# One sum of each feed-forward group made by an adding DMA transfer, and two more groups with a fourth step by seven

## The chip, the cores and the metric

The kernel runs on one core of a Trainium2 chip. The time is the device time of one execution in microseconds, taken as the median of three runs of the kernel before: 1799.47 us (1798.95 to 1800.05). Lower is better. A core has a matrix engine (TensorE, PE), VectorE (DVE), ScalarE (ACT), GpSimd (POOL), the sync engine that issues transfers (SyncE, SP), and 16 DMA engines that move data between memory (HBM) and the on-chip buffer (SBUF). TensorE accumulates into PSUM banks.

## What is computed

Two decoder layers over one sequence of 256 tokens of width 2048, in float32. Layer 0 mixes tokens by causal trailing means, layer 1 by differential attention. After each stands a dense feed-forward part, and that is where the change is:

```python
D_MODEL, SEQ, D_FF = 2048, 256, 5632

def swiglu(h, wg, wu, wd):
    return (jax.nn.silu(h @ wg) * (h @ wu)) @ wd

for i in range(2):
    h = h + mix(i, rmsnorm(h, norm_mix[i]))
    h = h + swiglu(rmsnorm(h, norm_ffn[i]), w_gate[i], w_up[i], w_down[i])
return rmsnorm(h, final_norm)
```

All weights are read from HBM once: three matrices of 2048 x 5632 in each of the two feed-forward parts, besides those of the mixers.

## The kernel before

**Precision.** Each operand is split into two halves, `hi` (the value rounded to the format that TensorE multiplies fast) and `lo` (what is left). A product is three matmuls: hi by hi, hi by lo, lo by hi. For weights ScalarE makes `hi` by a cast (L349 `whi`, L363 `thi`) and VectorE makes `lo` by a subtraction (L350 `wlo`, L364 `tlo`).

**Groups and steps.** `group()` computes one block of 256 x 1024 outputs. It runs over steps; a step is 256 rows of the weights by 1024 columns, stored in HBM as four blocks of 128 x 512 for each of 128 partitions in the order B12, B11, B22, B21 (1024 KB). A plain step is eight block products, 24 matmuls of 128 x 512. A **step by seven** replaces the eight products by seven products of sums (the Strassen-Winograd scheme), 21 matmuls. For that the weights have to be summed first, by `sums()` on VectorE:

- L355: `tsum0` = the pair (B11, B22) + B12, 128 x 1024
- L356: `tsum1[0]` = `tsum0[0]` + B22
- L357: `tsum1[1]` = `tsum1[0]` + B21

Then `tsum0` and `tsum1` are split like the weights (two L363 on ScalarE, two L364 on VectorE), and three of the four raw blocks by L349 and L350 (B12 is not used by itself). `prepared()` does all of this for one step: load, sums, halves. `products()` (L416) issues the matmuls, and `combined()` (L437 to L447) adds up the banks at the end of a group.

**Buffers.** `raw`, `whi` and `wlo` have three buffers each; `tsum0` and `tsum1` have one each, in the pool of the feed-forward part (`hp`). So a step by seven can write `tsum0` only when the one before it has been read by L356, L363 and L364.

**Loops.** `ffn(layer, ...)` runs over three chunks of 4, 4 and 3 gate/up groups. A gate/up group has eight steps over the 2048 inputs and gives 512 columns of gate and 512 of up; `GATE_UP[layer][g]` names its steps by seven. After each chunk follow two down groups of 8, 8 and 6 steps, whose steps by seven are 2, 4 and 6 as far as they go. The very last down group of layer 1 has none. The gate/up groups of both layers have the steps 2, 4, 5, 6 or 2, 4, 6 by seven; only the first of layer 0 has 4 and 6.

**Order.** The program isn't run in the order in which it is written. `in_order_of_need()` takes all instructions as `Step`s with a cost (`holds`: how long the engine is taken; `lasts`: how long until the result is there), walks them through the engines with a rank by need, up to eight times, keeps the shortest plan and fixes the order of TensorE, VectorE, ScalarE and SyncE by it. GpSimd's instructions stay in the order of the program. The costs are constants in the code: a load by SyncE holds it for 330 ns and lands after 2100 ns and 2500 ns per MiB, one transfer behind another. Each engine then executes its instructions strictly in the planned order; the one that waits holds up all behind it on its engine.

All weight loads go through SyncE's queue (L343), as do the transposing transfers of the activations (L515). GpSimd does nothing but a few set-up instructions at the start.

Of the kernel before, what the change touches and what calls it, by code (L numbers as in the profile page):

```python
# [10 lines left out]
F32 = mybir.dt.float32  # L11
# [3 lines left out]
ALU = mybir.AluOpType  # L15
# [3 lines left out]
P = 128  # L19
# [23 lines left out]

SEVEN = (2, 4, 5, 6)
SEVEN_DOWN = (2, 4, 6)
GATE_UP = [[(4, 6), (2, 4, 5, 6), (2, 4, 6), (2, 4, 5, 6), (2, 4, 5, 6), (2, 4, 5, 6), (2, 4, 6), (2, 4, 6), (2, 4, 5, 6), (2, 4, 5, 6), (2, 4, 6)], [(2, 4, 6), (2, 4, 5, 6), (2, 4, 6), (2, 4, 5, 6), (2, 4, 5, 6), (2, 4, 5, 6), (2, 4, 6), (2, 4, 6), (2, 4, 5, 6), (2, 4, 5, 6), (2, 4, 6)]]
SEVEN_QKV = (2, 4, 6)

EARLY = (tuple(range(NP)), (4, 6))
# [4 lines left out]
B12, B11, B22, B21 = range(4)  # L54
# [6 lines left out]
PE, DVE, ACT, SP, POOL = (mybir.EngineType.PE, mybir.EngineType.DVE, mybir.EngineType.Activation,  # L61
                          mybir.EngineType.SP, mybir.EngineType.Pool)
# [3 lines left out]
LANDING = 2100  # L66
# [4 lines left out]
class Step:  # L71

    def __init__(self, k, ins=None):
        self.k, self.ins, self.engine = k, ins, ins.engine if ins else POOL
        turns = bool(ins) and ins.opcode == "DmaTransposeAnt"
        self.dma = turns or bool(ins) and ins.opcode == "DMACopy"
        self.before, self.after, self.reads = set(), [], set()
        if not ins:
            self.holds = self.lasts = 0
            return  # L80
        size = lambda ap: math.prod(c for _, c in list(ap.ap)[1:])
        n = max(size(a) for a in list(ins.outs) + list(ins.ins) if hasattr(a, "ap"))
        if turns:
            self.share = TURN_TILE * n * P / 2048
            self.holds, self.lasts = 1290, 1000 + self.share
        elif self.dma:
            bytes_ = 4 * math.prod(c for _, c in ins.outs[0].ap)
            self.share = PER_MIB * bytes_ / 2 ** 20
            self.holds, self.lasts = (60 if self.engine == ACT else 330), LANDING + self.share
        elif self.engine == PE:  # L90
            n = size(ins.outs[0])
            one = 110 if ins.is_transpose else 14 + n / 2.4 if "float32r" in str(ins.ins[0].dtype) else 14 + n / 0.6
            self.holds, self.lasts = one, one + 163
        elif self.engine == DVE:
            if ins.opcode == "TensorScalarPtr":
                self.lasts = 185 + n / 0.96 if n > 8 else 159
            else:
                self.lasts = 152 + n / (1.92 if ins.opcode == "TensorCopy" else 0.96)
            self.holds = max(self.lasts - 80, 60)
        elif self.engine == ACT:  # L100
            self.lasts = 165 + n * 0.852
            if ins.opcode == "Activation" and any(hasattr(a, "ap") for a in list(ins.ins)[1:]):
                self.lasts += 100
            self.holds = max(self.lasts - 30, 60)
            if len(list(ins.ins[0].ap)) > 3:
                self.lasts += 80
            if len(ins.outs) > 1:
                self.lasts, self.holds = self.lasts + 190, self.lasts + 160
        else:
            self.holds = self.lasts = 400  # L110
# [168 lines left out]
def trunk_kernel(ctx, tc, x_n, gains, scale_in, final_in, subln, lam_in, band, counts_in, dist,  # L279
# [10 lines left out]
    nc = tc.nc  # L290
# [10 lines left out]
    def bank(i, shape=(P, 512)):  # L301
        return psum.tile(list(shape), F32, name=f"b{i}", tag=f"b{i}")
# [35 lines left out]
        return ap.bitcast(F32)  # L338


    def load(src):
        raw = wraw.tile([P, 4, 512], F32, name="raw")
        nc.sync.dma_start(out=raw, in_=src)  # L343
        return raw

    def halves(raw, lo_block=0):
        hi = whl.tile([P, 4, 512], F32R, name="whi")
        lo = whl.tile([P, 4, 512], F32R, name="wlo")
        nc.scalar.copy(hi[:, lo_block:], raw[:, lo_block:])  # L349
        nc.vector.tensor_tensor(lo[:, lo_block:], raw[:, lo_block:], f32(hi[:, lo_block:]), ALU.subtract)  # L350
        return hi, lo

    def sums(pool, raw):
        s, t = (pool.tile([P, 2, 512], F32, name=f"tsum{i}") for i in range(2))
        nc.vector.tensor_tensor(s, raw[:, B11:B22 + 1], raw[:, B12:B12 + 1].broadcast_to([P, 2, 512]), ALU.add)  # L355
        nc.vector.tensor_tensor(t[:, 0], s[:, 0], raw[:, B22], ALU.add)  # L356
        nc.vector.tensor_tensor(t[:, 1], t[:, 0], raw[:, B21], ALU.add)  # L357
        return s, t

    def sum_halves(pool, t, bufs, i):  # L360
        hi = pool.tile([P, 2, 512], F32R, name=f"thi{i}", bufs=bufs)
        lo = pool.tile([P, 2, 512], F32R, name=f"tlo{i}", bufs=bufs)
        nc.scalar.copy(hi, t)  # L363
        nc.vector.tensor_tensor(lo, t, f32(hi), ALU.subtract)  # L364
        return hi, lo
# [5 lines left out]
    def group(steps, pool, by_bank=0, bufs=1):  # L371


        plan = []
        for n, (a, seven, src) in enumerate(steps):
            if seven and n + 1 < len(steps) and steps[n + 1][1]:
                plan.append([(P5, [(S1, 1, 0)]), (M7, [(S3, 1, 1)]), (M6, [(S2, 2, 0)]), (P4, [(A22, 2, 1)]),
                             (M1, [(A11, 0, B11)]), (M2, [(A12, 0, B21)]), (P3, [(S4, 0, B22)])])
            elif seven:
                plan.append([(M1, [(A11, 0, B11)]), (M2, [(A12, 0, B21)]), (P3, [(S4, 0, B22)]), (P5, [(S1, 1, 0)]),  # L380
                             (M7, [(S3, 1, 1)]), (M6, [(S2, 2, 0)]), (P4, [(A22, 2, 1)])])
            else:
                plan.append([(C11, [((0, 0), 0, B11), ((1, 0), 0, B21)]), (C12, [((0, 0), 0, B12), ((1, 0), 0, B22)]),
                             (C21, [((0, 1), 0, B11), ((1, 1), 0, B21)]), (C22, [((0, 1), 0, B12), ((1, 1), 0, B22)])])
        left = {}
        for step in plan:
            for b, parts in step:
                left[b] = left.get(b, 0) + 3 * len(parts)
        ps = {}

        def prepared(seven, src):
            raw = load(src)
            t = sums(pool, raw) if seven else None
            w = [halves(raw, B11 if seven else 0)]
            if seven:
                w += [sum_halves(pool, t[i], bufs, i) for i in range(2)]
            return w

        def products(a, seven, w, b, parts):
            first = b not in ps  # L400
            if first:
                ps[b] = bank(b)
            for at, which, block in parts:
                hi, lo = w[which]
                if seven:
                    ah, al = a[:, 0, at], a[:, 1, at]
                else:
                    k, t = at
                    if a.shape[2] == 8:
                        slot = ((A11, A21), (A12, A22))[k][t]  # L410
                        ah, al = a[:, 0, slot], a[:, 1, slot]
                    else:
                        ah, al = (a[:, k, i, t * P:(t + 1) * P] for i in range(2))
                for x, y in ((ah, hi), (ah, lo), (al, hi)):
                    left[b] -= 1
                    nc.tensor.matmul(ps[b], x, y[:, block], start=first, stop=(left[b] == 0))  # L416
                    first = False

        head = len(steps) - by_bank
        for (a, seven, src), step in zip(steps[:head], plan[:head]):  # L420
            w = prepared(seven, src)
            for b, parts in step:
                products(a, seven, w, b, parts)
        if by_bank:
            ws = [prepared(seven, src) for a, seven, src in steps[head:]]
            for n in range(len(plan[head])):
                for (a, seven, src), step, w in zip(steps[head:], plan[head:], ws):
                    products(a, seven, w, *step[n])
        return ps
# [126 lines left out]
    with tc.tile_pool(name="start", bufs=1, reuse_waits="tile") as st:  # L556
# [27 lines left out]
        load_w(1, 0)  # L584
        load_w(1, 1)
        w_pool.append(load(pool_w[2]))
        nc.sync.dma_start(out=band_raw, in_=band)
        w_pool.append(load(pool_w[3]))
# [144 lines left out]
    def ffn(layer, xq, ss, next_op, next_gain):  # L733
# [3 lines left out]
        with tc.tile_pool(name=f"ffn{layer}", bufs=1, reuse_waits="tile") as hp:  # L737
            g0 = 0
            ys = []
            for c, n in enumerate(CHUNKS):  # L740
# [6 lines left out]
                for g in range(g0, g0 + n):  # L747

                    by_seven = GATE_UP[layer][g]
                    cs = combined(group([(xq[p], p in by_seven, w_gu[layer][g, p]) for p in range(NP)], hp), hp)  # L750
# [50 lines left out]
    with tc.tile_pool(name="attn", bufs=1, reuse_waits="tile") as ap_, ExitStack() as heads:  # L801
# [70 lines left out]
        for g in range(4):  # L872

            order, by_seven = LATE if g else EARLY
# [17 lines left out]
        for g in range(2):  # L892
            order, by_seven = LATE if g else EARLY
# [120 lines left out]
```

## Time and profile before

| | |
|---|---|
| median of three runs | 1799.47 us |
| the profiled execution, its time | 1799.01 us |
| its span, first to last instruction | 1797.2 us |
| granted TensorE clock, mean | 0.998 |
| L416 matmuls | 7491 |
| steps, of these by seven | 328, 127 |
| weight loads of 1024 KB by SyncE (L343) | 330 |

The page gives the busy time of each engine as a share of the span. A busy TensorE is not TensorE at its peak; how many matmuls start in a stretch of time says more, and who ended TensorE's waits says where another engine was late. A row of a group reads: line, engine, operation, output from inputs, shapes, count, then busy us and mean ns of one, then the idle time before it and what ended that.

### The profile page before, as it was taken

The page shows a single profiled execution, that of the slowest core. Times are in us where ns is not written, and L with a number is a line of the kernel's source. Part 1 is how long each engine was busy: PE and PEld are TensorE (multiplying, and loading weights), DVE is VectorE, ACT ScalarE, POOL GpSimd, SP SyncE. Part 2 cuts the span into 40 slices and gives each one's busy share as a digit, 9 for nine tenths or more (in the row PEclk, how much of TensorE's full clock was granted, in tenths as well). Part 3 has the DMA queues.
Part 4 walks back from the last instruction along what each step waited for, and adds up shares of the span by engine and source line. Part 5 has one row for each costly group of instructions (what it writes and reads, how often), then busy time and mean ns, then how long its engine had stood idle before and what let it go on. Part 6 is the DMA issues. An engine that isn't in the chain of part 4 may idle for free. (4 is left out here: it accounts for less than half of the span.)

```text
span 1797.2 us, 20952 instructions
## 1 busy us (share of the span) xinstructions
PE 1782.2 (99%) x7945; PEld 1467.4 (82%) x7945; DVE 1680.4 (94%) x1876; ACT 1184.0 (66%) x1294; POOL 0.7 (0%) x6
## 2 busy tenths in 40 slices
PE   9999999999999999999999999999999999999997
PEld 7888888888888888888888888888788888888886
DVE  7999999999999999998987889999999999999996
ACT  7676755666645678766666777676755766655773
POOL 0000000000000000000000000000000000000000
PEclk9999999999999999999999999999999999999999
DMA  7556655566655667644554464665655666566663
GB/s 267 211 204 223 226 208 193 199 243 203 223 209 204 206 201 231 215 175 164 187 186 174 179 199 176 216 230 198 223 213 207 210 214 227 206 223 215 217 211 117
DMA packets 105844, 369.99 MB, mean 206 GB/s; under 512 B 61072, under 2 KB 61200, under 8 KB 63376
## 3 DMA queue, kind: packets, MB, share of 16 engines
q1 hardware_dynamic: 104880, 367.03, 58.7%
q10 hardware_dynamic: 864, 1.63, 0.2%
q8 instruction: 62, 1.02, 0.2%
q14 instruction: 38, 0.31, 0.1%
HBM read 352.90 MB, written 2.10 MB: 198 GB/s over the span
## 5 line engine op out<-in xcount | busy, mean ns | idle before, releaser
L416 PE MATMUL b<-whi,xp 128*128 128x512 f32 x2654 | 849.3, 392 | 0.5 <-ACT e L529 0.2
L349 ACT CAST whi<-raw 128x1536 fp32r<-128x1536 f32 (+1 forms) x328 | 572.3, 1746 | 255.6 <-PE b L416 219.9
L350 DVE TENSOR_TENSOR wlo<-raw,whi 128x1536 fp32r<-128x1536 f32 (+1 forms) x328 | 681.6, 2078 | 55.5 <-ACT whi L349 53.8
L416 PEld LDWEIGHTS b<-whi,xp 128*128 128x128 f32 x2654 | 497.4, 188 | 103.7 <-ACT e L529 0.6
L416 PE MATMUL b<-wlo,xp 128*128 128x512 f32 x1327 | 519.8, 392 | 1.2 <-DVE wlo L350 1.2
L363 ACT CAST thi<-tsum 128x1024 fp32r<-128x1024 f32 x254 | 266.2, 1051 | 186.3 <-DVE tsum L355 61.5
L416 PE MATMUL b<-whi,h 128*128 128x512 f32 x1108 | 348.2, 389 | 0.7 <-DVE c L444 0.4
L364 DVE TENSOR_TENSOR tlo<-tsum,thi 128x1024 fp32r<-128x1024 f32 x254 | 306.2, 1217 | 4.9 <-ACT thi L363 4.6
L416 PEld LDWEIGHTS b<-wlo,xp 128*128 128x128 f32 x1327 | 249.3, 188 | 53.5 <-DVE wlo L350 2.8
L416 PE MATMUL b<-thi,xp 128*128 128x512 f32 x744 | 254.5, 389 | 0.0
L416 PEld LDWEIGHTS b<-whi,h 128*128 128x128 f32 x1108 | 207.9, 188 | 44.6 <-DVE c L444 0.9
L416 PE MATMUL b<-wlo,h 128*128 128x512 f32 x554 | 215.7, 389 | 0.0
L416 PEld LDWEIGHTS b<-thi,xp 128*128 128x128 f32 x744 | 139.6, 188 | 29.1
L355 DVE TENSOR_TENSOR tsum<-raw 128x1024 f32<-128x1024 f32 x127 | 154.5, 1216 | 1.5 <-DMA raw<-w_gu 1.5
L416 PE MATMUL b<-tlo,xp 128*128 128x512 f32 x372 | 145.0, 390 | 0.6 <-DVE tlo L364 0.6
L416 PEld LDWEIGHTS b<-wlo,h 128*128 128x128 f32 x554 | 104.0, 188 | 21.8 <-DVE wlo L350 0.2
L356 DVE TENSOR_TENSOR tsum<-tsum,raw 128x512 f32<-128x512 f32 x127 | 86.7, 683 | 0.4
L357 DVE TENSOR_TENSOR tsum<-tsum,raw 128x512 f32<-128x512 f32 x127 | 86.7, 683 | 0.2
L416 PEld LDWEIGHTS b<-tlo,xp 128*128 128x128 f32 x372 | 69.8, 188 | 16.0 <-DVE tlo L364 1.7
L416 PE MATMUL b<-thi,h 128*128 128x512 f32 x240 | 79.6, 389 | 0.0
L416 PE MATMUL b<-whi,oT 128*128 128x512 f32 x216 | 68.6, 394 | 0.0
L416 PEld LDWEIGHTS b<-thi,h 128*128 128x128 f32 x240 | 45.0, 188 | 9.4
(154 smaller groups left out, 1276.3 us busy)
## 6 DMA issues: line engine op xcount, KB each, us to landing
raw<-w_gu SPq DMA_DIRECT2D x176, 1024.0 KB, 4.9
raw<-w_down SPq DMA_DIRECT2D x88, 1024.0 KB, 4.8
raw<-w_qk SPq DMA_DIRECT2D x32, 1024.0 KB, 4.9
raw<-w_v SPq DMA_DIRECT2D x16, 1024.0 KB, 4.9
raw<-w_o SPq DMA_DIRECT2D x16, 1024.0 KB, 5.0
x_tok<-x_n SPq DMA_DIRECT2D x4, 512.0 KB, 7.3
w<-pool_w SPq DMA_DIRECT2D x4, 512.0 KB, 7.6
raw<-pool_w SPq DMA_DIRECT2D x2, 1024.0 KB, 11.7
```

The costliest lines, as they stand in the source:

```text
L349: nc.scalar.copy(hi[:, lo_block:], raw[:, lo_block:])
L350: nc.vector.tensor_tensor(lo[:, lo_block:], raw[:, lo_block:], f32(hi[:, lo_block:]), ALU.subtract)
L355: nc.vector.tensor_tensor(s, raw[:, B11:B22 + 1], raw[:, B12:B12 + 1].broadcast_to([P, 2, 512]), ALU.add)
L356: nc.vector.tensor_tensor(t[:, 0], s[:, 0], raw[:, B22], ALU.add)
L357: nc.vector.tensor_tensor(t[:, 1], t[:, 0], raw[:, B21], ALU.add)
L363: nc.scalar.copy(hi, t)
L364: nc.vector.tensor_tensor(lo, t, f32(hi), ALU.subtract)
L416: nc.tensor.matmul(ps[b], x, y[:, block], start=first, stop=(left[b] == 0))
```

## The change

In a feed-forward group the first step by seven no longer makes `tsum0` on VectorE. SyncE copies B12 twice from HBM into the two halves of `tsum0`, and GpSimd issues a transfer that reads B11 and B22 from HBM and adds them to what lies there. The load of `raw` leaves B12 out. L356 and L357 stay on VectorE. The later steps by seven of a group are as before, and so are all groups outside the feed-forward parts (their pool has another name).

Two gate/up groups of layer 0, 2 and 7, get a fourth step by seven, step 5. The planner learns the cost of a transfer issued by GpSimd: twice the time on the wire, 1100 ns for the issue, 1000 ns more until it lands.

```diff
-GATE_UP = [[(4, 6), (2, 4, 5, 6), (2, 4, 6), (2, 4, 5, 6), (2, 4, 5, 6), (2, 4, 5, 6), (2, 4, 6), (2, 4, 6), (2, 4, 5, 6), (2, 4, 5, 6), (2, 4, 6)], [
+GATE_UP = [[(4, 6), (2, 4, 5, 6), (2, 4, 5, 6), (2, 4, 5, 6), (2, 4, 5, 6), (2, 4, 5, 6), (2, 4, 6), (2, 4, 5, 6), (2, 4, 5, 6), (2, 4, 5, 6), (2, 4, 6)], [
...
             self.share = PER_MIB * bytes_ / 2 ** 20
-            self.holds, self.lasts = (60 if self.engine == ACT else 330), LANDING + self.share
+            if self.engine == POOL:
+                self.share *= 2
+            self.holds = {ACT: 60, POOL: 1100}.get(self.engine, 330)
+            self.lasts = LANDING + self.share + (1000 if self.engine == POOL else 0)
...
-    def load(src):
+    def load(src, first=0):
         raw = wraw.tile([P, 4, 512], F32, name="raw")
-        nc.sync.dma_start(out=raw, in_=src)
+        nc.sync.dma_start(out=raw[:, first:], in_=src[:, first:])
         return raw
...
-    def sums(pool, raw):
-        s, t = (pool.tile([P, 2, 512], F32, name=f"tsum{i}") for i in range(2))
-        nc.vector.tensor_tensor(s, raw[:, B11:B22 + 1], raw[:, B12:B12 + 1].broadcast_to([P, 2, 512]), ALU.add)
+    def sums(pool, raw, ready):
+        s = ready or pool.tile([P, 2, 512], F32, name="tsum0")
+        t = pool.tile([P, 2, 512], F32, name="tsum1")
+        if not ready:
+            nc.vector.tensor_tensor(s, raw[:, B11:B22 + 1], raw[:, B12:B12 + 1].broadcast_to([P, 2, 512]), ALU.add)
...
+    def sums_by_transfer(pool, src):
+        s = pool.tile([P, 2, 512], F32, name="tsum0")
+        nc.sync.dma_start(out=s, in_=src[:, B12:B12 + 1].broadcast_to([P, 2, 512]))
+        nc.gpsimd.dma_start(out=s, in_=src[:, B11:B22 + 1], accum_op=ALU.add)
+        return s
...
-        def prepared(seven, src):
-            raw = load(src)
-            t = sums(pool, raw) if seven else None
+        def prepared(seven, src, first=False):
+            by_transfer = seven and first
+            ready = sums_by_transfer(pool, src) if by_transfer else None
+            raw = load(src, B11 if by_transfer else 0)
+            t = sums(pool, raw, ready) if seven else None
...
-            w = prepared(seven, src)
+            first = pool.name.startswith("ffn") and seven and src is next(s for _, by_seven, s in steps if by_seven)
+            w = prepared(seven, src, first)
```

More of the change, by code (lines that the diff above doesn't have):

```diff
@@ L45 @@
 SEVEN_DOWN = (2, 4, 6)
-GATE_UP = [[(4, 6), (2, 4, 5, 6), (2, 4, 6), (2, 4, 5, 6), (2, 4, 5, 6), (2, 4, 5, 6), (2, 4, 6), (2, 4, 6), (2, 4, 5, 6), (2, 4, 5, 6), (2, 4, 6)], [(2, 4, 6), (2, 4, 5, 6), (2, 4, 6), (2, 4, 5, 6), (2, 4, 5, 6), (2, 4, 5, 6), (2, 4, 6), (2, 4, 6), (2, 4, 5, 6), (2, 4, 5, 6), (2, 4, 6)]]
+GATE_UP = [[(4, 6), (2, 4, 5, 6), (2, 4, 5, 6), (2, 4, 5, 6), (2, 4, 5, 6), (2, 4, 5, 6), (2, 4, 6), (2, 4, 5, 6), (2, 4, 5, 6), (2, 4, 5, 6), (2, 4, 6)], [(2, 4, 6), (2, 4, 5, 6), (2, 4, 6), (2, 4, 5, 6), (2, 4, 5, 6), (2, 4, 5, 6), (2, 4, 6), (2, 4, 6), (2, 4, 5, 6), (2, 4, 5, 6), (2, 4, 6)]]
 SEVEN_QKV = (2, 4, 6)
```

## The prediction

> **What bounds the kernel now.** The order of reading is: the busy line, the stretches of the two feed-forward layers, who keeps TensorE waiting, then whom VectorE waits for. The first fence has the busy line of the page and two rows of the view of stretches (columns: PE, PEld, DVE, ACT, POOL, each busy us and count; granted clock; DMA share; GB/s).
>
> ```profile
> span 1797.2 us, 20952 instructions
> PE 1782.2 (99%) x7945; PEld 1467.4 (82%) x7945; DVE 1680.4 (94%) x1876; ACT 1184.0 (66%) x1294; POOL 0.7 (0%) x6
> ...
> 57.00:722.00 665.00, 664.75 (x2933) 549.40 (x2932) 642.61 (x639) 442.95 (x420) 0.00 (x0) 1.00 0.62 214
> 1086.00:1745.00 659.00, 656.70 (x2899) 541.90 (x2899) 633.17 (x634) 425.99 (x399) 0.00 (x0) 1.00 0.61 211
> ```
>
> In the first layer TensorE starts 2933 matmuls in 665 us, one per 0.227 us, at full clock, and is short of work for 0.25 us. So TensorE is the bound, and it issues at an even beat; VectorE is busy for 97% of the same stretch and is the engine that would be the bound next. The waits of TensorE's weight loads, and three stretches of 50 us, show where VectorE comes too late:
>
> ```profile
> PEld b L416 <- DVE wlo L350: 2.9, 6, 1.4
> PEld b L416 <- DVE tlo L364: 1.7, 4, 1.0
> PEld b L416 <- DVE c L444: 1.4, 2, 0.9
> ...
> 350.00:400.00 50.00, 49.75 (x219) 40.67 (x218) 49.38 (x49) 36.36 (x35) 0.00 (x0) 1.00 0.68 236
> ...
> 1100.00:1150.00 50.00, 49.00 (x223) 40.41 (x222) 50.00 (x58) 33.59 (x38) 0.00 (x0) 1.00 0.57 211
> ...
> 1250.00:1300.00 50.00, 48.94 (x214) 39.50 (x213) 50.00 (x53) 36.34 (x35) 0.00 (x0) 1.00 0.66 218
> ```
>
> All waits of TensorE for VectorE's halves and combinations come to 6.0 us, a third of a per cent. That is nearly all there is to win besides matmuls. The chain that ended last crosses VectorE (L350, L442, L355, L444) at 1267 to 1272 us, and then runs on TensorE alone for 417 us:
>
> ```profile
> 1267.35 2.20 DVE wlo L350
> 1269.55 0.60 DVE c L442
> 1270.15 0.06 DVE tsum L355
> 1270.21 0.99 issue
> 1271.21 0.69 DVE c L444
> 1271.90 0.04 issue
> 1271.95 417.20 PE b L416 x1838
> ```
>
> **What the change removes.** The groups of VectorE, shapes apart, and one of TensorE that reads their result:
>
> ```profile
> L350 DVE TENSOR_TENSOR wlo<-raw,whi 128x2048 fp32r<-128x2048 f32 x201 | 459.4, 2285 | 46.4 <-ACT whi L349 45.2
> L364 DVE TENSOR_TENSOR tlo<-tsum,thi 128x1024 fp32r<-128x1024 f32 x254 | 306.2, 1217 | 4.9 <-ACT thi L363 4.6
> L350 DVE TENSOR_TENSOR wlo<-raw,whi 128x1536 fp32r<-128x1536 f32 x127 | 222.2, 1750 | 9.1 <-ACT whi L349 8.6
> L355 DVE TENSOR_TENSOR tsum<-raw 128x1024 f32<-128x1024 f32 x127 | 154.5, 1216 | 1.5 <-DMA raw<-w_gu 1.5
> L416 PE MATMUL b<-tlo,xp 128*128 128x512 f32 x372 | 145.0, 390 | 0.6 <-DVE tlo L364 0.6
> L356 DVE TENSOR_TENSOR tsum<-tsum,raw 128x512 f32<-128x512 f32 x127 | 86.7, 683 | 0.4
> ```
>
> Feed-forward groups with a step by seven: layer 0 has 11 gate/up and 6 down, layer 1 has 11 and 5 (its last has none): 33. Each loses one L355: 33 x 1.22 = 40 us of VectorE. Back to back an instruction costs about 0.08 us less than it lasts, as the starts of these rows show (2.20 between the first two, 2.27 for the two tlo of the second):
>
> ```profile
> 1380.96 2.29 DVE L350 TENSOR_TENSOR wlo<-raw,whi 128x2048 fp32r<-128x2048 f32 x1
> 1383.16 2.35 DVE L364 TENSOR_TENSOR tlo<-tsum,thi 128x1024 fp32r<-128x1024 f32 x2
> 1385.43 2.28 DVE L350 TENSOR_TENSOR wlo<-raw,whi 128x2048 fp32r<-128x2048 f32 x1
> ...
> 1393.56 1.22 DVE L355 TENSOR_TENSOR tsum<-raw 128x1024 f32<-128x1024 f32 x1
> ...
> 1395.89 0.68 DVE L356 TENSOR_TENSOR tsum<-tsum,raw 128x512 f32<-128x512 f32 x1
> ```
>
> So 33 x 1.14 = 38 us of occupied time goes.
>
> **What the two groups add.** A step by seven has 21 matmuls for 24: twice 3 fewer, 6 x 0.227 = **1.36 us off TensorE**. VectorE does 1.22 + 2 x 0.68 + 1.75 + 2 x 1.22 = 6.77 us for it, 6.3 occupied, against 2.2 for a plain step: 2 x 4.1 = 8.2 us more. VectorE ends some 29 us lighter, about 92% of the span.
>
> Where these fall matters. Groups 1 and 3 of layer 0 already have four sevens, and at the end of group 3 VectorE is hardly ahead: the last L350 ends at 201.90, and the matmul that reads a wlo starts 0.17 us later.
>
> ```profile
> 199.61 2.29 DVE L350 TENSOR_TENSOR wlo<-raw,whi 128x2048 fp32r<-128x2048 f32 x1
> ...
> 202.07 0.39 PE L416 MATMUL b<-wlo,xp 128*128 128x512 f32 x1
> ```
>
> With group 2 as dense as they are, VectorE over groups 1 to 3 gets 4.1 - 3 x 1.14 = 0.7 us more, and TensorE 0.7 us less to do: 1.4 us of lead lost, 0.2 there. I charge **+1.1 us** for a wait near 200 us (between 0, if other work is put later, and 1.4). In groups 4 to 7 the balance is 4.1 - 4 x 1.14, about -0.5 us, so group 7 is paid for.
>
> **What the lighter VectorE gives back.** The waits at 350 to 400 and 1250 to 1300 us come after a run of steps by seven; each such run now has 1.1 us per group less in it. I take the two stretches' missing time, 0.25 + 1.06 = **-1.3 us**. The longest wait for L350 (1.4 of the 2.9 us, in the stretch from 1100 us) stands ahead of layer 1's first step by seven and stays.
>
> **What the transfers cost.** Per first step: raw is 768 KB for 1024; tsum0 gets 512 KB by SP and 512 KB by GpSimd, which waits for the first. That is 768 KB more, 33 times, 26 MB:
>
> ```profile
> q1 hardware_dynamic: 104880, 367.03, 58.7%
> ...
> raw<-w_gu SPq DMA_DIRECT2D x176, 1024.0 KB, 4.9
> ...
> w<-pool_w SPq DMA_DIRECT2D x4, 512.0 KB, 7.6
> ...
> final_sb<-final_in ACTq DMA_DIRECT2D x2, 512.0 KB, 5.2
> out_t<-y SPq DMA_DIRECT2D x2, 512.0 KB, 3.3
> ...
> DMA to landing us min/median/max: 4.6/4.9/14.5
> ```
>
> The share of the DMA engines rises by 58.7 x 26/367, about 4 points, 7 if the sum also reads its target: room enough. Time is the question, since tsum0 has one buffer. The first transfer can start when the tlo that reads the old tsum0 is done, and L356 must now wait for the second. In the rows above that is 1383.16 + 1.2 to 1395.89: 11.5 us. There are 32 such intervals, 11.5 to 24.0 us; the last:
>
> ```profile
> 1710.08 2.35 DVE L364 TENSOR_TENSOR tlo<-tsum,thi 128x1024 fp32r<-128x1024 f32 x2
> ...
> 1729.49 0.68 DVE L356 TENSOR_TENSOR tsum<-tsum,raw 128x512 f32<-128x512 f32 x1
> ```
>
> 3 are under 12 us, 11 under 14, 19 under 16. No adding transfer and no GpSimd transfer is in this trace. Bounds: the first lands after 3.3 to 5.2 us (512 KB rows); the second after 3.3 at least, and 14.5 at most (the slowest load of all). I take 4.2 and 7.6 (the 512 KB loads that lie among others at the start, the nearest to a transfer that reads two operands): **X = 11.8 us**, ends 6.6 and 19.7. The planner's own figures in the code (330 + 2100 + 1250, then 1100 + 2100 + 2500 + 1000 ns) give 10.4, so it orders VectorE around that. At 11.8 one or two L356 wait 0.3 us, behind a lead of some us: **0**. Queued behind a late L356 is all of VectorE, so the two other sums, both thi on ScalarE, and then TensorE. Behind the SP transfer's wait stands the raw of step 1 or 2, whose own wait for a buffer ends at about the same time; ScalarE's waits for w_gu are small today:
>
> ```profile
> ACT whi L349 <- DMA raw<-w_gu: 14.4, 11, 3.0
> ```
>
> Nothing else is queued on GpSimd. SP issues 33 more at 0.33 us, hidden in its waits.
>
> The Trainium skill (DMA: Bandwidth & Descriptors, section on the anatomy of one DMA, GpSimd path) fits a plain transfer issued by GpSimd as 2.0 us plus bytes over 436 GB/s; by it, as an estimate, 512 KB take 3.2 us, X is 7.4 and the sum is the same. No run here shows it.
>
> **Sum**, against the profiled execution's 1799.01 us (span 1797.2 and 1.8 around it): -1.36 + 1.1 - 1.3 + 0 = -1.6, so 1797.4. The median shown, 1799.47, is 0.46 above that execution: **1797.9 us**. If the lighter VectorE bought nothing at all, and the lead held, it would be 1798.1, the same case.
>
> **The rivals.** *All of TensorE's waits for VectorE go* (faster): -1.36 - 6.0 at most, 1792.1; without that 1.4, 1793.5. For it: 29 us off an engine that is 97% busy. Against it: the planner makes a new order, and the dense groups at 200 us.
>
> *The pair of transfers is late* (slower): one mechanism, at L356. I set X against the 32 intervals, and took off 1.2 us and the smallest lead that a tlo has over its matmul in the next six steps (0.1 to 6 us, by counting the matmuls on tlo against the 254 rows of L364). TensorE loses 0 at X = 13, 2.5 us at 14, 7.4 at 15, 16 at 16, 43 at 18. It decides from about 14.5 us on. At 15: 1799.5 - 1.4 + 7.4 = 1805.5; at 16: 1814. For it: the 14.5 us row and TensorE's zero lead behind dense groups. Against it: a median of 4.9 us for twice the bytes, and at the tight places the planner can put other VectorE work first.
>
> *GpSimd's work on the transfer holds up VectorE, or VectorE holds it up* (slower): the trace has GpSimd idle, so nothing excludes it. At the planner's 1.1 us each, 33 x 1.1 = 36 us come back to VectorE, the saving is gone, and the two dense groups' 8.2 us meet no slack: 1799.5 - 1.4 + 8.2 = 1806. The Trainium skill (SBUF — State Buffer, section "Who interferes with whom") speaks for this rival in so far as one pair of ports is shared by both engines and locked for a whole instruction; it says of two-input VectorE sums, nearly all the work here, that they clash only with GpSimd instructions that read SBUF. No run here shows it.
>
> **Chances.** Forecast 0.55; all waits go 0.20; transfers late 0.17; GpSimd against VectorE 0.08. About 0.2% (3.6 us) is what a measurement of this kernel tells from no change, so the bounds are 1795.9 and 1803.1: faster 0.20, same 0.55, slower 0.25. The range runs from 1793 to 1810: it takes in nearly all of the first rival, and the slower ones up to X of about 15.5 us. The ends of X beyond that stay out; with them some 0.12 is left out. The likeliest case alone: 1796 to 1800.
>
> **What would show it.** Right: L355 94 times; matmuls of L416 7485; VectorE near 1650 us; TensorE short by under 0.5 us at 350 to 400 and 1250 to 1300, and a new wait of about 1 us at the end of group 3 near 200 us; L356 waiting for a transfer a handful of times, under 1 us each; two transfers of 512 KB landing after about 4 and 8 us. Wrong: VectorE waiting at L356 for the adding transfer in most of the 33 groups; VectorE's rows longer where GpSimd works; raw loads landing so late that ScalarE waits; waits of TensorE at places that this reading did not name.

## The result and the profile after

The changed kernel takes **1908.7 us** (median of four runs, 1906.5 to 1912.9); the kernel before took 1799.2 us beside it. The ratio is 1.061, 95% interval 1.0597 to 1.0622: slower by 109.5 us. The forecast was 1797.9 us with a range to 1810. The profiled execution took 1910.0 us with a span of 1908.2. One execution of all those below, of the kernel that is called tied, took 4693 us and is not counted.

The first lines of the page and the two main transfer queues:

```profile
span 1908.2 us, 21118 instructions
PE 1822.1 (95%) x7939; PEld 1478.7 (77%) x7939; DVE 1661.9 (87%) x1853; ACT 1184.2 (62%) x1298; POOL 29.6 (2%) x39
...
q1 hardware_dynamic: 113856, 375.69, 58.3%
q0 software_dynamic: 4752, 17.30, 4.9%
```

Six matmuls fewer were issued, as planned, yet TensorE was busy 40 us longer than before (1782.2) and idle for 86 us of its span instead of 15. A TensorE that is both busier and idler is one that waits and, besides, runs slower; both show below. VectorE's total went down from 1680.4 to 1661.9 us.

The waits (engine and line, whom it waited for, total us, times, longest):

```profile
ACT thi L374 <- DMA tsum<-w_gu: 100.7, 21, 12.9
...
ACT whi L352 <- DMA raw<-w_gu: 82.9, 27, 6.3
DVE tsum L361 <- DMA tsum<-w_gu: 55.3, 17, 6.2
...
ACT thi L374 <- DMA tsum<-w_down: 49.0, 11, 7.0
...
PEld b L429 <- ACT thi L374: 30.6, 20, 5.9
...
ACT whi L352 <- DMA raw<-w_down: 25.2, 12, 5.7
...
DVE tsum L361 <- DMA tsum<-w_down: 21.7, 7, 5.1
```

ScalarE's `thi` of the first step waits for the transfer into `tsum0` 32 times, VectorE's L361 (L356 before) 24 times, out of 33 groups. ScalarE also waits 83 us for `raw` of gate/up steps where it waited 14.4 us. The transfers (size, then median us from issue to landing):

```profile
raw<-w_gu SPq DMA_DIRECT2D x154, 1024.0 KB, 5.4
...
raw<-w_gu SPq DMA_DIRECT2D x22, 768.0 KB, 8.2
...
tsum<-w_gu SPq DMA_DIRECT2D x22, 512.0 KB, 6.6
tsum<-w_gu POOLq DMA_DIRECT2D x22, 512.0 KB, 8.6
```

The landing is counted from the start of the issue. From the copy's issue to the landing of the sum the 33 pairs took 15.7 us in the median (12.5 to 20.3); the plan counts 10.4. The first step's own load, with a quarter less to bring, lands 3.3 us later than a whole one did before (4.9).

One pair in the timeline (start us, us, engine line, operation; in brackets the idle time before and who ended it):

```profile
118.66 0.68 DVE L361 TENSOR_TENSOR tsum<-tsum,raw 128x512 f32<-128x512 f32 x1
...
119.40 0.38 SPq L367 DMA_DIRECT2D tsum<-w_gu  x1
...
121.57 3.74 SPq L346 DMA_DIRECT2D raw<-w_gu  x3
...
126.43 0.86 POOL L368 DMA_DIRECT2D tsum<-w_gu  x1 [43.20 <-DVE tlo L375]
...
128.38 1.92 ACT L352 CAST whi<-raw 128x2048 fp32r<-128x2048 f32 x1 [4.61 <-DMA raw<-w_gu]
...
132.67 0.49 PE L429 MATMUL b<-wlo,xp 128*128 128x512 f32 x1 [1.55 <-DVE wlo L353]
...
135.24 0.69 DVE L361 TENSOR_TENSOR tsum<-tsum,raw 128x512 f32<-128x512 f32 x1 [2.02 <-DMA tsum<-w_gu]
...
135.31 1.04 ACT L374 CAST thi<-tsum 128x1024 fp32r<-128x1024 f32 x1 [4.40 <-DMA tsum<-w_gu]
...
136.41 0.70 PE L429 MATMUL b<-thi,xp 128*128 128x512 f32 x1 [3.24 <-ACT thi L374]
```

SyncE issues the copy at 119.40, as soon as L361 of the step by seven before has read the old sum; 7.0 us later GpSimd issues the adding transfer; at 135.2 it has landed. ScalarE stands at `thi` for 4.40 us, VectorE at L361 for 2.02, and TensorE, fed by both, for 3.24. Before that, `whi` was 4.61 us late for the first of the three `raw` loads issued behind the copy; the three landed after 6.8, 8.0 and 9.6 us. Then follows something that the rows of before, with a clock of 1.00, do not show. Stretches of the same trace (PE, PEld, DVE, ACT, POOL, each busy us and count; granted clock; DMA share; GB/s):

```profile
57.00:762.00 705.00, 665.75 (x2843) 538.75 (x2842) 618.81 (x613) 423.36 (x396) 14.92 (x17) 0.98 0.67 212
...
136.40:139.80 3.40, 3.39 (x8) 2.72 (x9) 3.40 (x6) 3.01 (x3) 0.00 (x0) 0.52 0.32 130
139.90:143.30 3.40, 3.40 (x16) 2.79 (x15) 3.40 (x4) 0.00 (x0) 0.00 (x0) 0.99 0.43 128
```

From 136.40 TensorE is never idle, but its granted clock is 0.52 and 8 matmuls start where 16 do in the next stretch of the same length. The wait is over and still costs. The mean clock of the whole run is 0.984 against 0.998 before: 1908.2 x 0.016 - 1797.2 x 0.002 = 27 us at most of the 109.

### The profile page after: what moved, and what is told of

It reads as the page before. It is cut to its first block, busy times and chain, and to the rows that moved or that the text cites. A ratio compares the mean times of both kernels' runs of the same rounds, so it can differ in the third digit from the quotient of the medians.

```text
span 1908.2 us, 21118 instructions
## 1 busy us (share of the span) xinstructions
PE 1822.1 (95%) x7939; PEld 1478.7 (77%) x7939; DVE 1661.9 (87%) x1853; ACT 1184.2 (62%) x1298; POOL 29.6 (2%) x39
## 3 DMA queue, kind: packets, MB, share of 16 engines
q1 hardware_dynamic: 113856, 375.69, 58.3%
q0 software_dynamic: 4752, 17.30, 4.9%
## 5 line engine op out<-in xcount | busy, mean ns | idle before, releaser
L429 PE MATMUL b<-whi,xp 128*128 128x512 f32 x2634 | 857.2, 397 | 12.0 <-DVE c L459 8.0
L429 PEld LDWEIGHTS b<-whi,xp 128*128 128x128 f32 x2634 | 501.7, 191 | 121.0 <-DVE c L459 10.0
L429 PE MATMUL b<-wlo,xp 128*128 128x512 f32 x1317 | 522.3, 397 | 9.3 <-DVE wlo L353 9.3
L429 PE MATMUL b<-whi,h 128*128 128x512 f32 x1108 | 350.4, 392 | 8.1 <-DVE c L459 6.4
L375 DVE TENSOR_TENSOR tlo<-tsum,thi 128x1024 fp32r<-128x1024 f32 x258 | 310.1, 1217 | 9.1 <-ACT thi L374 8.9
L429 PEld LDWEIGHTS b<-wlo,xp 128*128 128x128 f32 x1317 | 251.4, 191 | 65.0 <-DVE wlo L353 13.1
L429 PE MATMUL b<-thi,xp 128*128 128x512 f32 x760 | 266.0, 397 | 20.7 <-ACT thi L374 20.7
L429 PEld LDWEIGHTS b<-whi,h 128*128 128x128 f32 x1108 | 208.9, 189 | 54.5 <-DVE c L459 7.3
L429 PE MATMUL b<-wlo,h 128*128 128x512 f32 x554 | 217.0, 392 | 3.1 <-DVE wlo L353 3.0
L429 PEld LDWEIGHTS b<-thi,xp 128*128 128x128 f32 x760 | 144.0, 190 | 55.9 <-ACT thi L374 27.6
L429 PE MATMUL b<-tlo,xp 128*128 128x512 f32 x380 | 151.6, 399 | 19.2 <-DVE tlo L375 19.1
L361 DVE TENSOR_TENSOR tsum<-tsum,raw 128x512 f32<-128x512 f32 x129 | 88.5, 686 | 77.7 <-DMA tsum<-w_gu 55.3
L429 PEld LDWEIGHTS b<-wlo,h 128*128 128x128 f32 x554 | 104.6, 189 | 27.1 <-DVE wlo L353 5.6
L360 DVE TENSOR_TENSOR tsum<-raw 128x1024 f32<-128x1024 f32 x96 | 116.9, 1217 | 2.9 <-DMA raw<-w_down 2.0
L429 PEld LDWEIGHTS b<-tlo,xp 128*128 128x128 f32 x380 | 71.9, 189 | 41.5 <-DVE tlo L375 26.6
L429 PE MATMUL b<-thi,h 128*128 128x512 f32 x240 | 79.1, 390 | 2.4 <-ACT thi L374 2.4
L429 PE MATMUL b<-whi,oT 128*128 128x512 f32 x216 | 68.9, 394 | 0.0
L429 PEld LDWEIGHTS b<-thi,h 128*128 128x128 f32 x240 | 45.0, 188 | 12.1 <-ACT thi L374 3.0
```

## The experiments

All ratios are to the kernel before, measured beside each. "The plan" is the length that the kernel's own planner works out for the order it fixes; it is a number of the code and no measurement: 1795.5 us for the kernel before (span 1797.2), 1795.0 for the changed one (span 1908.2). So the changed kernel runs 113 us longer than its plan, the one before 1.7.

**The two parts apart.** One kernel has the two new groups and makes all sums on VectorE, the other has the transfers and the old list of groups.

```diff
-            by_transfer = seven and first
+            by_transfer = False
```

> The two denser gate/up groups alone; every first step makes its sum on VectorE again. Late transfers (theory): nothing of the 109 us is left, 1797 to 1802 us, L361 never waits for a transfer, granted clock 0.998. Too dense groups (rival): at least a quarter of the loss stays, above 1825 us.

> The 33 adding transfers alone, with the groups of before. Late transfers: 1895 to 1915 us, L361 and thi wait for the transfers some 220 us in total, granted clock 0.985. Too dense groups: within 10 us of before.

Measured: groups only 1800.0 us (1.0003, 0.9994 to 1.0012); transfers only 1906.4 us (1.0594, 1.0578 to 1.061). The groups neither gain nor cost anything that can be measured; the transfers are the whole loss, as the first theory had it.

**The plan told of the pair.** First the copy and the adding transfer are each planned longer (SyncE's copy 3.5 us, GpSimd's transfer 1.8 us more).

```diff
-            self.lasts = LANDING + self.share + (1000 if self.engine == POOL else 0)
+            self.lasts = LANDING + self.share + (2800 if self.engine == POOL else 0)
+            if self.engine == SP and bytes_ == 2 ** 19 and "tsum0" in str(getattr(ins.outs[0], "bass_ap").tensor.name):
+                self.lasts += 3500
```

> The change, but the planner reckons with what the trace of after shows: 3.5 us more for the copy of B12, 1.8 us more for the adding transfer, so about 15.7 us from the release of tsum0 for 10.4. Plan built on a time that is too short (theory): the order now leaves the room, waits at L361 and thi fall below 60 us, 1800 to 1825 us; by the intervals of before (11.5 to 24 us) some of the loss stays. Traffic (rival: the 16 engines are too busy and the raw loads land late): the order does not help, above 1880 us.

Measured 1860.4 us (1.0336, 1.0322 to 1.0351): 48 us come back, which lies between the two expectations. The plan is now 1853.9 and the span 1858.8, so the order comes out nearly as planned, but it is a long order.

The same with one constant: the whole correction put on GpSimd's transfer, 6300 (a pair of 15.7 us), or 8000 (17.4 us), in place of 1000.

```diff
-            self.lasts = LANDING + self.share + (1000 if self.engine == POOL else 0)
+            self.lasts = LANDING + self.share + (6300 if self.engine == POOL else 0)
```

> The change with one constant changed: a transfer issued by GpSimd lands 5.3 us later in the planner's reckoning, so that the pair takes 15.7 us there, as the trace of after shows, with all of it booked on the second transfer. The planner's own end for this order is 1807 us (1795 for the change, 1854 for e3, which booked the same total on both transfers). Wrong cost in the planner (theory): 1808 to 1825 us, L361 and thi wait under 60 us. Traffic (rival): above 1860 us, as e3.

> As e14, with 17.4 us for the pair; the planner's own end is 1810 us. Wrong cost: within 8 us of e14 and fewer waits at L361 and thi, since the slowest pairs of after (17 to 18 us) are now allowed for. Traffic: above 1860 us, the same as e14.

Measured 1834.2 us (1.0188, 1.0167 to 1.0208) and 1840.0 us (1.0227, 1.021 to 1.0244). **One constant of the planner takes 74.5 of the 109.5 us away**, with every transfer, byte and instruction still there. That is 9 us above the theory's range and 26 below the rival's. How much comes back also depends on the order that the planner happens to find: the same 15.7 us, split over both transfers, gave a plan of 1853.9 us, and here 1807.3; why, was not followed up. The waits of the first of the two, and two rows of its transfers:

```profile
ACT whi L352 <- DMA raw<-w_gu: 50.2, 20, 5.2
...
ACT whi L352 <- DMA raw<-w_down: 20.0, 9, 4.1
PEld b L429 <- DVE wlo L353: 19.5, 17, 2.1
...
ACT thi L374 <- DMA tsum<-w_down: 12.1, 5, 4.1
...
ACT thi L374 <- DMA tsum<-w_gu: 9.4, 3, 5.7
```

```profile
raw<-w_gu SPq DMA_DIRECT2D x22, 768.0 KB, 7.7
...
tsum<-w_gu POOLq DMA_DIRECT2D x22, 512.0 KB, 8.7
```

`thi` waits 8 times for the pair where it did 32 times, 21.5 us where it did 150, though the adding transfer takes as long as ever (8.7). The mean clock of this execution, the fastest of the four, is back at 0.998; the others have 0.993 to 0.997. What is left stands in the first three rows shown: ScalarE waits 70 us for `raw`, and VectorE's `wlo` behind it is late for TensorE. Plan 1807.3, span 1825.9: 12 us are in the order itself, 18.6 were not foreseen. With 17.4 us the plan is 1810.3 and the span 1838.0.

**No adding at all.** One plain 512 KB transfer by GpSimd takes the place of the pair, planned at its first guess and then at 1.6 us less.

```diff
-        nc.sync.dma_start(out=s, in_=src[:, B12:B12 + 1].broadcast_to([P, 2, 512]))
-        nc.gpsimd.dma_start(out=s, in_=src[:, B11:B22 + 1], accum_op=ALU.add)
+        nc.gpsimd.dma_start(out=s, in_=src[:, B11:B22 + 1])
```

> Leaves out the copy of B12 and the addition: tsum0 gets B11 and B22 by one plain transfer of GpSimd (512 KB), no transfer waits for another; VectorE has the same work as after. Chain of two transfers too long (theory): the chain is 6 to 9 us, shorter than the 10.4 that the planner reckons with for the pair, so 1796 to 1806 us and no waits at L361. Traffic (rival): 512 KB less per first step of the 768 KB that were added, so a third of the loss stays, about 1835 us. GpSimd against VectorE (rival): VectorE's rows of 1217 and 2286 ns get longer; theory: they do not.

> As e8 (one plain transfer, no copy, no addition: the result leaves B12 out), with the planner's cost of it brought down to the 5.1 us measured. The planner's own end is 1800 us, 1806 for e8. If e8's 24 us come from the order that the planner found: 1800 to 1812 us. If they come from traffic: 1820 us or more, as e8.

Measured 1823.6 us (1.0135, 1.0121 to 1.0149) and 1826.3 us (1.0155, 1.014 to 1.017). Even without the copy and without adding, VectorE's saved 38 us buy nothing and 24 us are lost. The theory's 1796 to 1806 us is missed. In the first of the two the rows that grew are again those of loads (two of its waits, then two of its transfers and its second queue; before, the same waits came to 8.3 and 14.4 us):

```profile
ACT e L536 <- DMA turned<-c: 39.4, 12, 5.3
ACT whi L352 <- DMA raw<-w_gu: 36.0, 18, 4.7
```

```profile
q0 software_dynamic: 4752, 17.30, 2.7%
...
raw<-w_gu SPq DMA_DIRECT2D x22, 768.0 KB, 6.2
...
tsum<-w_gu POOLq DMA_DIRECT2D x22, 512.0 KB, 5.1
```

A lower price in the plan did not help: planned 6 us shorter (1799.9 for 1805.9), the kernel was no faster. `whi` waits less for gate/up loads (13.8 us for 36.0), `thi` more for the transfer (30.4 for 8.4), which lands after 5.7 us in this order. By the second expectation this speaks for traffic; the tied kernel below says how much bytes alone cost.

**A buffer of its own.** The pair writes a buffer that it need not wait for. Room for it was made by one step by seven less in each down group; that control alone takes 1807.2 us (1.0042, 1.0027 to 1.0057).

```diff
-SEVEN_DOWN = (2, 4, 6)
+SEVEN_DOWN = (2, 4)
...
-        s = pool.tile([P, 2, 512], F32, name="tsum0")
+        s = pool.tile([P, 2, 512], F32, name="tsumx")
```

> The control of the next three: the kernel before with the down groups' step 6 made plain (SEVEN_DOWN = (2, 4)), which frees 4 KB of SBUF per partition. 8 down groups get 3 matmuls more: 24 x 0.227 = 5.4 us, so 1803 to 1806 us, all theories alike.

> The change on the control, and the sum made by transfer has a buffer of its own (tsumx), so that the two transfers can start most of a group ahead. One buffer, too short an interval (theory): L361 and thi hardly wait for the transfers (under 10 us in total), 1800 to 1812 us, granted clock 0.998. Traffic (rival: the transfers delay the raw loads): raw loads still land after 7 us and more where the transfers run, ScalarE still waits some 100 us for raw, 1840 us or more.

> As e10, and the planner reckons with the measured times of both transfers. One buffer: as e10 within 5 us, since with a group's time ahead the planner's error no longer matters. Planner's error alone (rival): e10 still loses 20 us or more and this one does not.

Measured 1867.6 us (1.0378, 1.0363 to 1.0394), and with the longer costs in the plan 1911.6 us (1.0626, 1.0605 to 1.0647). The buffer was not the cure: against its control the first still loses 60 us, as the traffic rival had it in time. Its waits and a row of its transfers say where:

```profile
ACT e L543 <- DMA turned<-c: 37.0, 9, 7.9
ACT whi L352 <- DMA raw<-w_gu: 33.6, 21, 3.8
DVE tsum L360 <- DMA raw<-w_gu: 32.2, 22, 5.6
...
ACT e L537 <- DMA turned<-c: 28.0, 11, 6.9
```

```profile
raw<-w_gu SPq DMA_DIRECT2D x154, 1024.0 KB, 6.5
```

The pair is early now (`thi` waits 8.7 us for it on gate/up steps), and what is late are other loads of SyncE: the whole `raw` loads of gate/up land after 6.5 us for 4.9, and the turned activations are waited for 65 us. The first steps' own 768 KB loads are not late here: 4.6 us. With the longer costs most of the further loss is in the order itself: its plan is 1847.5 us long, that of the first 1801.8; the spans are 1916.4 and 1864.2. Neither expectation for the second held.

**The bytes without a reader.** Three kernels make all sums on VectorE and run the transfers into a buffer that nobody reads. In the first, which also has the two denser groups, the planner places them. In the second they were meant to lie beside the control's own order, each behind its first step's `whi`, all on GpSimd's queue.

> The control with both transfers into tsumx, which nobody reads; raw is loaded in full and VectorE makes every first sum itself. So it has all of the traffic (256 KB more than the change per first step) and none of the waits. One buffer: within 10 us of the control. Traffic: 40 us or more above the control. GpSimd against VectorE: VectorE's rows longer than 1217 and 2286 ns.

> The control of e9 in its own order (the planner does not see what is added), with the copy of B12 and the adding transfer issued by GpSimd alone into a buffer that nobody reads, one pair in each group with a step by seven, started when the first such step's whi is there. All of the traffic and GpSimd's work, 256 KB more than the change per step, no wait for it and SyncE's queue as before. Traffic (rival): 25 us or more above the control's 1807. Theory: within 8 us of it. GpSimd against VectorE: VectorE's rows longer than in e9.

Measured 1928.2 us (1.0708, 1.069 to 1.0726) and 2007.9 us (1.1159, 1.1143 to 1.1176). Both are misses, since in both a queue stood still for a reason of its own. The row of the first, then three of the second (a wait and two stretches):

```profile
SPq L367 <- DMA tsumx<-w_gu: 233.4, 22, 12.9
```

```profile
ACT whi L351 <- POOL gate L364: 182.6, 6, 39.3
```

```profile
100.00:150.00 50.00, 24.15 (x93) 18.85 (x92) 20.94 (x20) 17.23 (x18) 6.64 (x9) 0.73 0.66 160
300.00:1200.00 900.00, 899.12 (x3990) 732.26 (x3989) 805.85 (x945) 583.77 (x677) 6.99 (x13) 1.00 0.57 199
```

In the first, the pairs did not run one per group: they stood one behind the other at the start of each layer (57 to 295 us, 1185 to 1404 us), so SyncE's next copy waited up to 12.9 us for the previous adding transfer to land, with all `raw` loads behind it. In the second the transfers were not tied to their step and ran as two bursts (before 300 us and from 1200 us on). GpSimd, waiting for one to land before it issued the next, came late to the small copy that ScalarE's next `whi` waited for: six stops of up to 39.3 us are nearly the whole loss. Neither says what the bytes cost.

The third, the tied kernel, ties them: GpSimd first writes one element of the step's `whi` into the buffer that the transfer then overwrites.

```diff
+        s = pool.tile([P, 2, 512], F32, name="tsumx")
+        nc.gpsimd.tensor_copy(s[:, 0, 0:1], f32(hi[:, B11, 0:1]))
+        nc.gpsimd.dma_start(out=s, in_=src[:, B12:B12 + 1].broadcast_to([P, 2, 512]))
+        nc.gpsimd.dma_start(out=s, in_=src[:, B11:B22 + 1], accum_op=ALU.add)
```

> The control (one step by seven less in each down group, 1807.2 us) with the bytes of the change beside it and no reader: at each of the 33 first steps GpSimd first copies one element of that step's whi into the unread buffer, then issues the plain transfer and the adding transfer into it, so that a pair runs once per group and after its first step, on no queue but GpSimd's. VectorE makes all its sums as before. The planner is told 8.5 us for each transfer and nothing of a load on the DMA engines; its plan is 1798.5 us long, the control's 1799.9. If what remains of the loss with the right pair time (some 25 us of 35) is traffic on the DMA engines that slows raw and turned loads wherever the pair lies, this is 1820 to 1835 us, with raw of 1024 KB landing above 5.5 us in the median. If traffic alone costs nothing and the remainder is that the first step's own transfers and loads land together and are late for their own readers, it is within 5 us of the control, 1803 to 1812, raw near 5.0 us.

Measured 1812.7 us (1811.9 to 1816.5; 1.0067, 1.0046 to 1.0087). Against the control's 1.0042 that is 0.25%, some 4 us, with intervals that meet; by the medians it is 5.5, by the profiled spans (1814.7 and 1805.2) 9.5. That is between the two expectations, and nearer to the cheap one. Its transfers, and the stretch through the first feed-forward part, the control's and then its own:

```profile
q0 software_dynamic: 9504, 34.61, 9.4%
...
raw<-w_gu SPq DMA_DIRECT2D x176, 1024.0 KB, 5.1
...
tsumx<-w_gu POOLq DMA_DIRECT2D x44, 512.0 KB, 6.6
```

```profile
57.00:727.00 670.00, 667.89 (x2942) 550.87 (x2941) 625.32 (x613) 433.55 (x409) 0.00 (x0) 1.00 0.62 212
...
57.00:727.00 670.00, 665.53 (x2928) 548.00 (x2926) 619.07 (x607) 426.87 (x402) 41.33 (x51) 1.00 0.74 235
```

With 35 MB more than the control and a DMA share of 0.74 in the first layer (0.62 in the control), `raw` lands after 5.1 us (4.8 in the control) and TensorE starts 2928 matmuls in 670 us, 14 fewer. So these bytes cost 4 to 10 us when they are off SyncE's queue, behind the step's own loads and without a reader. The loss is not bandwidth as such; it comes from how the transfers are placed and waited for. Which of the three counts, the queue, the place or the reader, this run does not separate.

**The plan told of the load as well.** The kernel with the pair at 15.7 us, and the 768 KB loads planned 3.5 us longer too.

```diff
+            if bytes_ == 786432:
+                self.lasts += 3500
```

> The change with the pair planned at 15.7 us as in the run before (1834.2 us, span 1825.9, 18.6 us above its plan of 1807.3), and the 768 KB loads of the first steps planned 3.5 us longer as well, near the 7.7 us that they took there. The plan is now 1877.2 us long. If the 18.6 us were these loads being late against the plan, the measured span is within 8 us of the plan: 1872 to 1885. If something else that the plan does not know costs as much (other transfers slowed, the clock), the gap stays: 1892 to 1900. A span below the plan by more than 5 us would say that the loads come sooner when they are not planned against each other.

Measured 1877.7 us (1.0429, 1.0414 to 1.0445), span 1875.9 against a plan of 1877.2. The gap of 18.6 us between plan and span is gone, as it should be if these loads were what the plan had missed. That does not prove it: the kernel with the price split over both transfers also has a gap of only 4.9 us, with no word of the loads in its plan, and both have a longer plan. The order is worse, too: ScalarE still waits 89 us for `raw`, and the plan with these loads in it is 1877 us long, while the one without runs in 1826. A plan with more of the delays in it is not the shortest run here.

## Why the prediction was wrong

**The matmuls: right in count, without effect.** L429 has 7485 matmuls, as said, and the two groups alone moved the time by 0.5 us with an interval of -1.1 to 2.2. The sum had -1.36 + 1.1 for them, which lies inside.

**VectorE's saving: there, and smaller in the total.** L355's group went from 154.5 us to 116.9 us for L360 (96 times; the prediction's 94 left out the two new steps). The total fell by 18.5 us to 1661.9, where 29 and about 1650 were forecast; where the other 10 or so went was not followed up. Nothing of the saving reached the end. The -1.3 us for recovered waits is not shown by any run: the groups-only kernel keeps VectorE's work, and every kernel with transfers that VectorE reads is slower by 24 us or more.

**GpSimd against VectorE: no.** This rival's sign would have been longer rows of VectorE. They are as before:

```profile
L353 DVE TENSOR_TENSOR wlo<-raw,whi 128x2048 fp32r<-128x2048 f32 x199 | 454.8, 2286 | 69.8 <-ACT whi L352 68.9
L375 DVE TENSOR_TENSOR tlo<-tsum,thi 128x1024 fp32r<-128x1024 f32 x258 | 310.1, 1217 | 9.1 <-ACT thi L374 8.9
```

2286 and 1217 ns, against 2285 and 1217. The rule of the Trainium skill weighed there (SBUF — State Buffer, "Who interferes with whom": a two-input VectorE sum clashes only with a GpSimd instruction that reads SBUF) agrees with that: the instructions that the change gives GpSimd are the 33 issues of L368, whose source is HBM.

**The step that failed is X, "What the transfers cost", twice over.** Its size first: 4.2 + 7.6 = 11.8 us was taken; the copy landed after 6.5 and the adding transfer after 8.6, and with the time between them the pair took 15.7, inside the bounds of 6.6 and 19.7 that the text gave. The copy was priced from 512 KB rows elsewhere in the run (3.3 to 5.2 us), but it is issued in front of other loads and lands among them. A plain 512 KB transfer by GpSimd, 3.2 us by the prediction's estimate, landed after 5.1 and 5.7 us in the two kernels that have one. Second, and larger: X was set against the 32 intervals **of the old order**, where 13 of 32 are at least 16 us wide. The planner makes a new order, and it puts L361 and `thi` where its own 10.4 us end. The text knew both facts ("so it orders VectorE around that") and still charged the old intervals. Against the plan the median group is then late by 15.7 - 10.4 = 5.3 us, whatever gap there had been: `thi` waits in 32 of 33 groups, 4.7 us on the mean. Spread over the groups, the 109.5 us, late loads and clock included, are 3.3 us each. The rival named the right mechanism, but its table priced X = 16 at 16 us, a seventh of what came, for this reason. The runs with other constants show it: the same X, planned, costs 35 us with the price on one transfer and 61 with it split, and not 109; span and plan are 19 and 5 us apart, and not 113.

**Who waits.** The text put VectorE first behind a late L356. It is ScalarE: `thi` of `tsum0` stands in ScalarE's order in front of the next `whi`, and waits 150 us in all, twice what VectorE waits at L361.

**"Room enough" and the raw behind SyncE's copy, charged at 0.** In bytes that was nearly right (4 to 10 us for more bytes than the change moves, in the tied kernel). In time it was wrong: 768 KB land after 8.2 us, ScalarE's waits for gate/up loads go from 14.4 to 82.9 us, and with the pair planned at 15.7 us on one transfer this is the largest wait of TensorE, VectorE or ScalarE for a transfer that remains (50.2).

**The clock wasn't in the sum at all.** Up to 27 us of the 109 are TensorE at half speed after a wait, a consequence of the waits that no term allowed for.

What stays open: how the last 35 us divide. In the profiled execution, the fastest, the order accounts for 12 and 18.6 were not foreseen. Late loads are the likely reason, since the plain transfer alone still costs 24 us with the same waits grown; which transfer delays which load was not separated. No version here beats the kernel before.

## What to carry to other kernels

Where a planner fixes the order, a transfer of a new kind is late against **the planner's figure**, not against the gaps of the old trace: compare its measured time with the planned one, multiply by the number of places for a rough upper mark (5.3 x 33 = 175 us here; 109.5 came), and treat the old gaps as gone. Price a transfer from rows in which it lies among the same neighbours, and count what is queued behind it. Here an engine that was 97% busy off the path was not worth relieving with transfers in front of the loads that the path waits for.

## What the runs showed of the hardware

**Half clock after windows that are half empty.** Cut the trace of the changed kernel into windows of 3.413 us, counted from 136.53 us, where the slow piece shown above begins. Sixteen of them have a granted clock of 0.50, and all the others close to 1.00. The sixteen form twelve stretches; in the window before each stretch TensorE was busy between 0% and 53% of the time, and after no window above that did the clock fall from full. One such pair:

```profile
1495.04:1498.45 3.41, 1.81 (x8) 0.95 (x6) 2.75 (x4) 3.38 (x5) 0.00 (x0) 1.00 1.00 351
1498.45:1501.87 3.42, 3.42 (x9) 2.68 (x10) 3.42 (x3) 3.39 (x5) 0.00 (x0) 0.50 0.43 180
```

The Trainium skill (TensorE: Matmul & The Clock Gate, Part 1) puts half rate behind an idle window of about 3.4 us that runs freely. The length agrees; that the window must be idle does not, since here one busy for 1.81 of its 3.41 us was enough. A window with 1.73 us of work (from 542.7 us) was not followed by half clock, so the limit lies near one half; this profile does not give it more sharply.

**An adding transfer is dear for the DMA engines.** Queue q0 moved 17.30 MB in 4.9% of 16 engines' span, 5.4 us per MB; q1 took 58.3% for 375.69 MB, 3.0 us per MB: 1.8 times per byte. The plain transfers by GpSimd moved the same 17.30 MB on the same queue in 2.7% of a span of 1822.5 us, 2.8 us per MB, so the higher price goes with the adding and not with GpSimd's queue. Landing was 8.6 us against 5.1 for the plain transfer of the same size by GpSimd.
